# A split-fp32 input projection on TensorE: seven products of block sums in place of eight, in two halves of the contraction

## The chip, the cores and the metric

The kernel runs on one core of one Trainium2 chip. Times are device microseconds (us) of one execution. The core's engines each run their own instruction stream in order: TensorE (PE in the rows; PEld is its weight load), VectorE (DVE), ScalarE (ACT), GpSimd (POOL), and SyncE (SP), whose stream issues nearly all DMA transfers.

## The reference

One decoder layer for 1,024 tokens of width 2,048. A first product gives everything that two parallel branches need, and two more products and a layer norm close the layer. All of it is float32.

```python
mod = c @ w_ada[i] + b_ada[i]
shift, scale, gate = jnp.split(mod, 3, axis=-1)
h = _ln(x) * (1.0 + scale[:, None, :]) + shift[:, None, :]
proj = h @ w_in[i]
q, kv, ng, za, us, zb, ga, gb = jnp.split(proj, offs, axis=-1)
o_a = _nsa(q, kv, jax.nn.sigmoid(ng), rel_bias, ...) * jax.nn.silu(za)
o_b = _s5(us, ssm_a_re[i], ...) * jax.nn.silu(zb)
m = jax.nn.sigmoid(ga) * (o_a @ w_branch_nsa[i]) + jax.nn.sigmoid(gb) * (o_b @ w_branch_ssm[i])
x = _ln(DEEPNORM_ALPHA * x + gate[:, None, :] * (m @ w_out[i])) * ln_g[i] + ln_b[i]
```

`w_in` is 2,048 by 9,776: 76 tiles of 128 output columns, and 48 columns `ng`. `_nsa` is sparse attention (16 heads in 4 groups, compressed, selected and window parts), `_s5` a state-space layer (64 groups of 16 channels, an associative scan over the tokens).

## The kernel before, in words

**Number format.** Each float32 operand is split into a rounded `hi` (a cast on ACT) and the rest `lo` (a subtraction on DVE, L113). A product is three matmuls: hi x hi, hi x lo and lo x hi.

**Input projection.** `h` lies in SBUF, transposed, as 16 pairs of tiles `hhi[k]`, `hlo[k]` of 128 x 1,024. `dense` (L238) computes one tile of 128 output columns for all tokens in two PSUM banks (`dps`): four units of weights come in (`w_unit`, 256 KB each, split on ACT and DVE), each serves four `k`, and `mm6` issues six matmuls of 128 x 512 per `k`: 96 a tile. 73 tiles run so. Three more (`acc`) are accumulated in the startup, while `w_ada`'s shift and scale part (64 tiles `wa` of 512 KB) still arrives. `dense_ng` computes the 48 gate columns in 64 matmuls. An evacuation function per kind of tile (`ev_us`, `ev_q`, `ev_k`, `ev_v`, ...) writes the result to DRAM.

**Stages.** After the startup come eight state-space blocks (`Ssm.block`), each put behind two or three dense tiles; then `compress` (the compressed keys and values); then attention units (`Attention.unit`, one group of heads and one block of 128 queries). `EARLY` says how many of the eight query blocks of each group are computed early, on top of the dense tiles that are left; the other ones run late, on top of the output products. A scheduler orders the instructions of each engine by priority and by when buffers come free. Weights are loaded and split at a raised priority, so the dense matmuls fill the gaps of the other work.

**A state-space block** is a chain over the engines: `rot` (powers of a rotation, built by doubling on DVE), X (`sps<-U,et`, PE), rotations and scans on DVE, Y (`sps<-e,v`, PE), a trip of `y` through DRAM that reorders it (`y_d`, then the tile `gy`), the GELU, and the store of `U`. The tiles `rot0` and `rot1` have buffers of their own; `bank()` gives the block's PSUM tiles from a pool of four, which `ev_v` and `compress` use too.

Of the kernel before, what the change touches and what calls it, by code (L numbers as in the profile page):

```python
# [27 lines left out]
EARLY = (6, 6, 6, 4)  # L28
# [22 lines left out]
def _hybrid(es, tc, A, out):  # L51
# [33 lines left out]
    mb_d = [scratch(f"mb_d{i}", [128, 512]) for i in range(16)]  # L85

# [11 lines left out]
    stp = es.enter_context(tc.tile_pool(name="st", bufs=3))  # L98


    p1 = ExitStack()
    xh = p1.enter_context(tc.tile_pool(name="xh", bufs=32, side="right"))

    def w_unit(src, shape=[128, 4, 128], rp=None):

        raw = (rp or wp).tile([128, 512], F32, name="wraw", tag="wraw", bufs=3 if rp else WR)
        if len(shape) == 3:
            raw = raw.rearrange("p (k c) -> p k c", k=4)
        ld(raw, src)
        hi = wp.tile(shape, F32R, name="whi", tag="whi")  # L110
# [5 lines left out]
    hhi, hlo = [None] * KT, [None] * KT  # L116
    w_in = A["w_in"]

    def mm6(ps, k, hi, lo, ku):
        a = k == 0  # L120
        z = k == KT - 1
        for hf in range(2):
            c = slice(512 * hf, 512 * hf + 512)
            PE.matmul(ps[hf], hi[:, ku], hhi[k][:, c], start=a, stop=False)  # L124
            PE.matmul(ps[hf], hi[:, ku], hlo[k][:, c], start=False, stop=False)  # L125
        for hf in range(2):
            c = slice(512 * hf, 512 * hf + 512)
            PE.matmul(ps[hf], lo[:, ku], hhi[k][:, c], start=False, stop=z)  # L128

# [3 lines left out]
    sc_cm = tc.tile_pool(name="sc", bufs=1)  # L133
    sc = sc_cm.__enter__()
    cP = sc.tile([128, KT, 32], F32, name="cP")
    ld(cP, A["c"])
    ssm = Ssm(nc, tc, A, sc, ident, ld, rd, st_)
    sct_cm = tc.tile_pool(name="sct", bufs=1)
    sct = sct_cm.__enter__()
    s0 = ExitStack()  # L140
    p0 = s0.enter_context(tc.tile_pool(name="p0", bufs=1))
    pp = s0.enter_context(tc.tile_pool(name="pp0", bufs=1, space=PSUM))

    NS = 3
    units = []


    def load_wa(n):
        wa = (stp if n % 7 % 2 else p0).tile([128, 2, 512], F32, name="wa", tag="stg" if n % 7 % 2 else "wa", bufs=3 if n % 7 % 2 else 4)
        ld(wa, A["w_ss"][n // 8][:, 2 * (n % 8):2 * (n % 8) + 2])  # L150
        return wa

    xn, was = [], {}
    for b in range(NB):
        t = xh.tile([128, T], F32, name=f"xa{b}", tag="xh"), xh.tile([128, T], F32, name=f"xb{b}", tag="xh")
# [14 lines left out]
        if b > 1:  # L170
            was[b - 2] = load_wa(b - 2)
    xs = [(p0 if k == KT - 1 else xh).tile([128, T], F32, name=f"x{k}", tag="x15" if k == KT - 1 else "xh")
          for k in range(KT)]
    for hf in range(2):
        for k in range(KT):
            tp = pp.tile([128, 512], F32, name="tp", tag="st", bufs=6)
# [4 lines left out]
    for k in range(0, KT, 2):  # L181
        mp = pp.tile([128, 512], F32, name="mp", tag="mp", bufs=2)
        for n in range(8):
            wa = was.pop(4 * k + n) if 4 * k + n in was else load_wa(4 * k + n)
# [3 lines left out]
        pm = p0.tile([128, 512], F32, name="pm", tag="pm", bufs=1)  # L188
        S.copy(pm, mp)
        for i in range(4):  # L190
# [3 lines left out]
        if k % 4 == 0:  # L194
            units.append([w_unit(w_in[TILES["us"][i]][:, k:k + 4]) for i in range(NS)])

    acc = [[pp.tile([128, 512], F32, name="acc", tag="st", bufs=6) for _ in range(2)] for _ in range(NS)]
    for k in range(KT):
        V.tensor_scalar(xs[k], xs[k], mods[:, k, 0:1], mods[:, k, 1:2], op0=MUL, op1=ADD)
        hhi[k] = xh.tile([128, T], F32R, name=f"hhi{k}", tag="xh")  # L200
        S.copy(hhi[k], xs[k])
        hlo[k] = xh.tile([128, T], F32R, name=f"hlo{k}", tag="xh")
        V.tensor_tensor(hlo[k], xs[k], f(hhi[k]), op=SUB)
        for i in range(NS):
            mm6(acc[i], k, *units[k // 4][i], k % 4)

    ssm.tables(sct)


    def ev_us(ps, i):  # L210
        s = stage()
        sv_ = s.rearrange("p (s m) -> p s m", s=8)
        for hf in range(2):
            S.copy(sv_[:, :, 64 * hf:64 * hf + 64], ps[hf].rearrange("p (m s) -> p s m", s=8))
        st_(us_d[i].rearrange("s c g m -> (c g) s m"), sv_)

    for i in range(NS):
        ev_us(acc[i], i)
    s0.close()
    sct_cm.__exit__(None, None, None)  # L220

    psa = es.enter_context(tc.tile_pool(name="psa", bufs=2, space=PSUM))
    psb = p1.enter_context(tc.tile_pool(name="psb", bufs=2, space=PSUM))
    turn = [0]

    def psum_a():
        return psa.tile([128, 512], F32, name="pa", tag="d")

    def pair():
        turn[0] ^= 1  # L230
        return [(psa if turn[0] else psb).tile([128, 512], F32, name="dps", tag="d") for _ in range(2)]

    pss_cm = tc.tile_pool(name="pss", bufs=4, space=PSUM)
    pss = pss_cm.__enter__()

    side = iter(())

    def dense(wi, ev, *a):  # L238
        ps = pair()
        for u in range(4):  # L240
            with tc.high_priority(offset=WPRI):
                hi, lo = w_unit(w_in[wi][:, 4 * u:4 * u + 4])
            for ku in range(4):
                mm6(ps, 4 * u + ku, hi, lo, ku)
            next(side, None)
        ev(ps, *a)
# [4 lines left out]
    def ev_cin(ps, i):  # L251
        s = stage()
        v = s.rearrange("p (b m) -> p b m", b=16)
        for hf in range(2):
            S.copy(v[:, :, 32 * hf:32 * hf + 32], ps[hf].rearrange("p (m b) -> p b m", b=16))
        st_(cin_d[i], v)

    def ev_split(ps, scale):
        hi, lo = stage(F32R), stage(F32R)
        for hf in range(2):  # L260
            c = slice(512 * hf, 512 * hf + 512)
            S.mul(hi[:, c], ps[hf], scale)
            V.scalar_tensor_tensor(lo[:, c], ps[hf], scale, f(hi[:, c]), op0=MUL, op1=SUB)
        return f(hi), f(lo)

    def ev_q(ps, i):
        hi, lo = ev_split(ps, -0.125)
# [5 lines left out]
    def ev_k(ps, w, i):  # L273
        hi, lo = ev_split(ps, 1.0)
# [4 lines left out]
    def ev_v(ps, w, i):  # L279
        s = stage()  # L280
        for hf in range(2):
            S.copy(s[:, 512 * hf:512 * hf + 512], ps[hf])
        for hf in range(2):
            tp = bank()
            for b in range(4):
                PE.transpose(tp[:, 128 * b:128 * b + 128], s[:, 512 * hf + 128 * b:512 * hf + 128 * b + 128], ident[:, :128])
# [7 lines left out]
    def ev_silu2(ps, dst):  # L294
        s = stage()
        for hf in range(2):
            c = slice(512 * hf, 512 * hf + 512)
# [1135 lines left out]
```

## Time and profile before

| what | value |
|---|---|
| median of 3 runs | 3238.25 us (3235.42 to 3239.47) |
| the profiled execution's own time | 3234.84 us |
| span of its profile | 3233.1 us |
| PE busy | 3162.2 us, 98% |
| DVE busy | 1686.2 us, 52% |
| ACT busy | 1127.2 us, 35% |
| POOL busy | 85.5 us, 3% |
| moved by DMA | 432.21 MB, 134 GB/s over the span |

The shares are means over stages that differ: in a stage an engine can be full that is half idle over the whole. The granted clock of TensorE over the span is 0.991 of full speed.

### The profile page before, as it was taken

To read this page: it belongs to the slowest core of one execution; us is meant where nothing else is said; L and a number is where in the kernel's file an instruction comes from. 1 tells how busy PE (TensorE), PEld (TensorE's weight loads), DVE (VectorE), ACT (ScalarE), POOL (GpSimd) and SP (SyncE) were. 2 spreads that over 40 slices of the span, in tenths; PEclk is the share of its full clock that TensorE was granted. 3 is DMA by queue.
4 is the path that set the end of the run, shared out by engine and by line. 5 is a ranking of instruction groups with operands and counts; after the bars stand their busy time and mean duration, and the time that the engine had idled before them with its cause. 6 is when DMAs were issued, how large, how long until landed. Compare 5 with 4: busy or idle time off the path is not lost.

```text
span 3233.1 us, 43112 instructions
## 1 busy us (share of the span) xinstructions
PE 3162.2 (98%) x15603; PEld 2538.1 (79%) x15603; DVE 1686.2 (52%) x4615; ACT 1127.2 (35%) x2327; POOL 85.5 (3%) x66
## 2 busy tenths in 40 slices
PE   7999999999999999999999999999999999999896
PEld 4467788888888888888888888887888888788784
DVE  8354678763444434334333334426777665534737
ACT  4212222222433334333433234325555443322323
POOL 0000000000000000000000000000000000000302
PEclk9999999999999999999999999999999999999998
DMA  9654524344322232222322222236668444734533
GB/s 335 236 170 147 172 94 141 103 128 119 117 92 74 77 97 88 71 64 83 97 77 74 67 84 91 76 126 202 213 207 285 142 131 147 241 114 144 166 119 138
DMA packets 286398, 432.21 MB, mean 134 GB/s; under 512 B 40324, under 2 KB 139428, under 8 KB 286184
## 3 DMA queue, kind: packets, MB, share of 16 engines
q1 hardware_dynamic: 286184, 429.45, 41.0%
q8 instruction: 123, 2.02, 0.3%
q14 instruction: 91, 0.75, 0.1%
HBM read 331.30 MB, written 98.05 MB: 133 GB/s over the span
## 4 chain that ended last, share of the span: by engine, by line
PE 93%; DVE 3%; DMA 2%; ACT 1%; issue 1%; SPq 0%; ACTq 0%; DVEq 0%
PE dps L124 17%; PE dps L125 17%; PE dps L128 17%; PE po L957 5%; PE ps L814 4%; PE pt L935 4%; PE pa L462 4%; PE pa L463 4%; PE pa L464 4%; PE e L602 2%; PE e L601 2%; PE e L603 2%; PE mp L187 2%; DVE r L595 1%; PE acc L124 1%; PE e L462 1%
## 5 line engine op out<-in xcount | busy, mean ns | idle before, releaser
L124 PE MATMUL dps<-hhi,whi 128*128 128x512 f32 x2336 | 927.8, 397 | 0.0
L125 PE MATMUL dps<-hlo,whi 128*128 128x512 f32 x2336 | 925.2, 396 | 0.0
L128 PE MATMUL dps<-hhi,wlo 128*128 128x512 f32 x2336 | 750.3, 396 | 0.0
L111 ACT CAST whi<-wraw 128x512 fp32r<-128x512 f32 x544 | 336.2, 619 | 1054.9 <-PE dps L125 622.7
L113 DVE TENSOR_TENSOR wlo<-wraw,whi 128x512 fp32r<-128x512 f32 x544 | 381.0, 701 | 600.9 <-ACT whi L111 587.8
L124 PEld LDWEIGHTS dps<-hhi,whi 128*128 128x128 f32 x2336 | 439.7, 188 | 103.8 <-issue 13.0
L125 PEld LDWEIGHTS dps<-hlo,whi 128*128 128x128 f32 x2336 | 439.8, 188 | 93.7 <-issue 7.0
L128 PEld LDWEIGHTS dps<-hhi,wlo 128*128 128x128 f32 x2336 | 433.4, 188 | 92.5 <-issue 5.7
L940 DVE TENSOR_TENSOR ptl<-pt,pth 128x512 fp32r<-128x512 f32 (+2 forms) x320 | 204.1, 646 | 269.3 <-ACT pth L939 267.6
L939 ACT CAST pth<-pt 128x512 fp32r<-128x512 f32 (+2 forms) x320 | 172.0, 552 | 456.7 <-PE pt L935 456.0
L462 PE MATMUL pa<-op,whi 128*128 128x512 f32 x528 | 210.0, 400 | 2.1 <-ACT op L449 1.7
L463 PE MATMUL pa<-op,whi 128*128 128x512 f32 x528 | 209.7, 397 | 2.5 <-DMA op<-oa_d 2.5
L464 PE MATMUL pa<-op,wlo 128*128 128x512 f32 x528 | 208.8, 396 | 0.0
L602 PE MATMUL e<-wlo,m 128*128 128x512 f32 x368 | 148.0, 402 | 9.9 <-DVE rsd L42 5.4
L603 PE MATMUL e<-whi,m 128*128 128x512 f32 x368 | 146.3, 398 | 0.0
L929 ACT ACTIVATE psl<-psl,mn 128x128 f32<-128x128 f32 (+7 forms) x128 | 99.2, 775 | 81.3 <-DVE mn L842 80.5
L601 PE MATMUL e<-whi,m 128*128 128x512 f32 x368 | 122.0, 401 | 0.6 <-ACT whi L111 0.6
L462 PEld LDWEIGHTS pa<-op,whi 128*128 128x128 f32 x528 | 99.8, 189 | 23.3 <-ACT op L449 3.3
L463 PEld LDWEIGHTS pa<-op,whi 128*128 128x128 f32 x528 | 99.6, 189 | 22.9 <-DMA op<-oa_d 2.9
L464 PEld LDWEIGHTS pa<-op,wlo 128*128 128x128 f32 x528 | 99.6, 189 | 20.1 <-issue 0.7
L904 POOL TENSOR_TENSOR near<-bn,msk 128x512 f32<-128x512 f32 x32 | 35.1, 1098 | 2662.1 <-DVE msk L900 2535.9
L883 ACT ACTIVATE pw<-pw,mn 128x640 f32<-128x640 f32 (+4 forms) x128 | 88.9, 694 | 32.4 <-DVE mn L842 31.6
(308 smaller groups left out, 4271.1 us busy)
## 6 DMA issues: line engine op xcount, KB each, us to landing
wraw<-in_w_in SPq DMA_DIRECT2D x304, 256.0 KB, 3.0
wraw<-in_w_out SPq DMA_DIRECT2D x136, 256.0 KB, 3.0
wa<-in_w_ss SPq DMA_DIRECT2D x64, 512.0 KB, 5.7
wg<-in_w_gate SPq DMA_DIRECT2D x32, 512.0 KB, 3.6
q<-q_d SPq DMA_DIRECT2D x64, 256.0 KB, 4.1
wraw<-in_w_bn SPq DMA_DIRECT2D x64, 256.0 KB, 3.1
q_d<-stg SPq DMA_DIRECT2D x32, 256.0 KB, 3.9
oa_d<-ptl SPq DMA_DIRECT2D x64, 128.0 KB, 2.2
```

The source lines that it names most:

```text
L111: S.copy(hi, raw)
L113: V.tensor_tensor(lo, raw, f(hi), op=SUB)
L124: PE.matmul(ps[hf], hi[:, ku], hhi[k][:, c], start=a, stop=False)
L125: PE.matmul(ps[hf], hi[:, ku], hlo[k][:, c], start=False, stop=False)
L128: PE.matmul(ps[hf], lo[:, ku], hhi[k][:, c], start=False, stop=z)
L462: PE.matmul(ps, hi[:, j], x[k][0], start=k == 0, stop=False)
L463: PE.matmul(ps, hi[:, j], x[k][1], start=False, stop=False)
L464: PE.matmul(ps, lo[:, j], x[k][0], start=False, stop=k == 7)
L601: PE.matmul(a, mk[0][:, t], hi, start=k == 0, stop=False)
L602: PE.matmul(a, mk[0][:, t], lo, start=False, stop=False)
L603: PE.matmul(a, mk[1][:, t], hi, start=False, stop=k == KT - 1)
L940: V.tensor_tensor(lo[0:n, :w], tp[0:n, :w], f(hi[0:n, :w]), op=SUB)
```

## The change

Two output tiles and two tiles of `k` form blocks of a 2 x 2 product, with the two token halves as the other side. `dense(pair, half, last)` computes a pair of output tiles over one half of the contraction (8 of 16 `k`, four 2 x 2 blocks `j`) by seven products (`PRODUCTS`) of sums of weight blocks with sums of `h` blocks. The sums of `h` (`combine`) are formed once, 28 tiles `hc` of 512 KB for a half, and only one half's are in SBUF; both halves' lie in DRAM (`hc_d`), and `fetch_h` reads 28 of them over the 28 that are in use. The weight sums (`weights`) are formed for each pair and half on POOL, and each of the seven is split. The first half's result of a pair goes to DRAM (`pt_d`) and is read back and added by the second.

The order becomes: the startup forms scale and shift for half of `k`, and the other half between the first four pairs; 18 pairs `one` (us, the compress inputs, k, v, q, za) over half 0; `ng` and the position table; `fetch_h(1)`; the 18 pairs over half 1, with a state-space block behind every second of the first 16; `ng`; `compress`; then 20 pairs `two` over half 1, `fetch_h(0)`, and 20 over half 0, two steps to each of 20 early attention units. `EARLY` goes from 22 units to 20. `compress` splits its weights in the buffers of `dense`, and `rot` shares the buffer `gy`.

```diff
-EARLY = (6, 6, 6, 4)
+EARLY = (5, 5, 5, 5)
...
+    def fetch_h(half):
+        for i, _, _ in PRODUCTS:
+            for j in range(4):
+                d = hc[i, j] = hcp.tile([128, 2, 512], F32R, name="hc", tag="hc")
+                rd(f(d), hc_d[half][j][i])
+
+    def weights(wis, half):
...
+        P.tensor_tensor(s3, a11, a21, op=SUB)
+        yield w_split(a11)
+        P.tensor_tensor(a11, a22, s3, op=SUB)
+        yield w_split(a11)
+        P.tensor_tensor(a21, a21, a22, op=ADD)
+        yield w_split(a21)
+        yield w_split(s3)
+        P.tensor_tensor(a11, a12, a11, op=SUB)
+        yield w_split(a11)
+        yield w_split(a12)
+        yield w_split(a22)
+
+    def product(ps, i, hi, lo, first):
+        for j in range(4):
+            bh, bl = hc[i, j][:, 0], hc[i, j][:, 1]
+            PE.matmul(ps, hi[:, j], bh, start=first and j == 0, stop=False, skip_group_check=True)
+            PE.matmul(ps, hi[:, j], bl, start=False, stop=False, skip_group_check=True)
+            PE.matmul(ps, lo[:, j], bh, start=False, stop=j == 3, skip_group_check=True)
+
+    def dense(pair, half, last):
...
+        for n, (i, b, first) in enumerate(PRODUCTS):
+            with tc.high_priority(offset=WPRI):
+                hi, lo = next(w)
+            if first:
+                ps[b] = dbank()
+            product(ps[b], i, hi, lo, first)
+            if n == 1:
+                S.copy(s1, ps["a"])
+                if last:
+                    u2 = acc()
+                    V.tensor_tensor(u2, ps["b"], s1, op=ADD)
+                    P.tensor_tensor(c12, c12, u2, op=ADD)
...
+    for n in range(n_one):
+        dense(one[n], 1, True)
+        if n % 2:
+            b = n // 2
+            if b < 8:
+                ssm.block(sp, bank, b, us_d[b], y_d[b], y2_d[b], stage)
...
+        work = [(p, 1, False) for p in two]
+        work += [None] + [(p, 0, True) for p in two]
...
+            att.unit(qb)
+            while n < (u + 1) * len(work) // len(early):
+                step()
...
-        R = [tl(f"rot{i}", [128, 4, 128]) for i in range(2)]
+        rot = tl("gy", [128, 2, 4, 128])
+        R = [rot[:, i] for i in range(2)]
```

Before, PE's stream through a state-space block (here from one block's X, `sps<-U,et`, past its Y, `sps<-e,v`, to the first row of the next block) reads so; every `dps` row is a dense matmul:

```order
L1266 MATMUL sps<-ident,ka 128x128 [waits DVE_49]
...
L1274 MATMUL sps<-U,et_3557 64x128 x7
L128 MATMUL dps<-hhi_1135,wlo 128x512 x2
...
L1320 MATMUL sps<-U,w_3581 128x128 [waits Activation_49]
L128 MATMUL dps<-hhi_1158,wlo 128x512 x2
L124 MATMUL dps<-hhi_1181,whi 128x512
...
L1321 MATMUL sps<-e_3676,v_3538 128x127 [waits DVE_49]
...
L124 MATMUL dps<-hhi_1388,whi 128x512
...
L1252 MATMUL sps<-ident,e_4025 128x128 x3
```

After, the stretch from block 1's Y (`v_5595`) through the whole of block 2 (`e_6091` to `v_6100`) and block 3 up to its X (`et_6638`), to the transposes of `ev_v` (`sps<-ident,stg`), reads so. The rows left out are rows of the same lines:

```order
L210 MATMUL dps<-hc,wlo 128x512
L1462 MATMUL sps<-e_5732,v_5595 128x127 [waits DVE_49]
...
L1392 MATMUL sps<-ident,e_6091 128x128 [waits DVE_49]
...
L1414 MATMUL sps<-U,et_6118 64x128 [waits DMAHW3_49,PE_49]
...
L1462 MATMUL sps<-e_6236,v_6099 128x127 [waits DVE_49]
...
L1392 MATMUL sps<-ident,e_6611 128x128 [waits DVE_49]
...
L1414 MATMUL sps<-U,et_6638 64x128 [waits DMAHW3_49,PE_49]
...
L371 MATMUL sps<-ident,stg 128x128 [waits DMAHW7_49,DVE_49,PE_49]
...
L208 MATMUL dps<-hc,whi 128x512
```

Of its 84 rows none is a dense matmul: what stood between the blocks has moved ahead of the first row and behind the last. The same holds from the last `ng` matmul (L409) on: the rest of block 6, all of block 7 and all of `compress` (L834 to L862) stand in 152 rows without a dense one.

```order
L409 MATMUL dps<-hc,whl 128x512 x25
L1462 MATMUL sps<-e_8368,v_8231 128x127 [waits DVE_49]
...
L1392 MATMUL sps<-ident,e_8731 128x128 [waits DVE_49]
...
L1414 MATMUL sps<-U,et_8758 64x128 [waits DMAHW1_49,PE_49]
...
L1462 MATMUL sps<-e_8876,v_8739 128x127 [waits DVE_49]
...
L836 MATMUL sps<-cth,wlo 128x264
L208 MATMUL dps<-hc,whi 128x512 [waits Activation_49]
```

Before, the matmuls of the last block and of `compress` stand in pieces of at most 24 rows between dense rows. At the end of the early attention, too, the order moves: before, 161 dense matmuls stand behind the last row of the last early unit; after, the last dense row stands ahead of 274 rows of the last four early units, and then the output products begin (`pa<-op`).

On SP, `fetch_h(1)` stands behind the partial sums' stores; `hc<-hc_d` are its transfers, `wr` the weights, `wg` another weight:

```order
L261 DMA pt_d_274<-stg 128x1024 [waits DMAHW1_49,DVE_49,Pool_49]
L182 DMA hc<-hc_d_0_245 128x1024 [waits DMAHW2_49,PE_49]
L182 DMA hc<-hc_d_1_246 128x1024 [waits DMAHW3_49,PE_49]
L182 DMA hc<-hc_d_2_247 128x1024 [waits PE_49]
L182 DMA hc<-hc_d_3_248 128x1024 [waits DMAHW5_49,PE_49]
L456 DMA wg<-in_w_gate 128x4x256 [waits DMAHW7_49,DMAHW6_49]
L456 DMA wg<-in_w_gate 128x4x256 [waits DMAHW1_49]
L189 DMA wr<-in_w_in 128x1024 [waits DMAHW0_49,DVE_49,Pool_49]
```

Each `hc` transfer waits for PE to be done with the tile that lies in its buffer. Before, there is no such row: `hhi` and `hlo` stay where they are.

## Rows read from the trace of the kernel before

**Rows 1.** The page: busy time and share, busy tenths of 40 slices.

```profile
PE 3162.2 (98%) x15603; PEld 2538.1 (79%) x15603; DVE 1686.2 (52%) x4615; ACT 1127.2 (35%) x2327; POOL 85.5 (3%) x66
...
DVE  8354678763444434334333334426777665534737
```

**Rows 2.** Busy time by stretch: stretch, length, PE, PEld, DVE, ACT, POOL, clock, DMA share, GB/s.

```profile
0.00:160.00 160.00, 140.28 (x659) 70.54 (x660) 99.52 (x393) 54.69 (x86) 0.20 (x4) 0.98 0.82 287
0.00:40.00 40.00, 20.28 (x112) 12.27 (x114) 32.62 (x103) 18.98 (x33) 0.20 (x4) 0.96 0.92 341
220.00:700.00 480.00, 480.00 (x2704) 377.90 (x2704) 339.42 (x850) 109.27 (x191) 0.00 (x0) 1.00 0.42 132
780.00:2180.00 1400.00, 1400.00 (x6835) 1160.56 (x6835) 539.83 (x1718) 503.19 (x1174) 13.59 (x12) 1.00 0.26 85
```

**Rows 3.** Timeline of PE: start, duration, line, tile.

```profile
1900.62 0.39 PE L124 MATMUL dps<-hhi,whi 128*128 128x512 f32 x1
...
1901.53 0.63 PE L128 MATMUL dps<-hhi,wlo 128*128 128x512 f32 x2
```

**Rows 4.** DVE's and PE's groups from 220 to 700 us: busy, mean ns.

```profile
L113 DVE TENSOR_TENSOR wlo<-wraw,whi 128x512 fp32r<-128x512 f32 x70 | 48.2, 688 | 38.1 <-ACT whi L111 37.1 <-issue 0.3
L263 DVE SCALAR_TENSOR_TENSOR stg<-dps,stg 128x512 fp32r<-128x512 f32 x10 | 6.5, 682 | 0.0
...
L124 PE MATMUL dps<-hhi,whi 128*128 128x512 f32 x558 | 222.4, 399 | 0.0
...
L365 PE MATMUL sps<-wg,cP 128*32 128x256 f32 x232 | 18.5, 391 | 0.0
```

**Rows 5.** Timeline of DVE, one block's X to the next one's X.

```profile
511.98 0.69 DVE L1193 TENSOR_TENSOR t<-sps,rot 128x512 f32<-128x512 f32 x1 [2.18 <-PE sps L1274]
...
524.89 0.69 DVE L1193 TENSOR_TENSOR e<-t,t 64x512 f32<-64x512 f32 x1
...
541.41 1.23 DVE L1193 TENSOR_TENSOR w<-gy 128x1024 f32<-128x1024 f32 x1 [1.77 <-DMA gy<-y_d]
...
544.70 0.24 DVE L1193 TENSOR_TENSOR t<-rot,up 128x4 f32<-128x4 f32 x2
...
548.20 2.25 DVE L1338 SCALAR_TENSOR_TENSOR U<-w,gy 128x1024 f32<-128x1024 f32 x1
...
560.53 0.42 DVE L1193 TENSOR_TENSOR rot<-t,t 128x256 f32<-128x256 f32 x1
...
563.96 0.69 DVE L1193 TENSOR_TENSOR t<-sps,rot 128x512 f32<-128x512 f32 x1 [2.16 <-PE sps L1274]
```

**Rows 6.** Timelines of SP and PE: last block's store, first matmul of `compress`.

```profile
718.33 0.33 SPq L1340 DMA_DIRECT2D y_d<-U  x1
757.73 0.28 PE L694 MATMUL sps<-cth,cwh 128*128 128x264 f32 x1
```

**Rows 7.** Timelines of DVE and POOL near 3030 us.

```profile
3022.11 4.79 DVE L595 TENSOR_TENSOR r<-r,ln_g 128x512 f32<-128x512 f32 x4
3033.74 1.57 DVE L113 TENSOR_TENSOR wlo<-wraw,whi 128x512 fp32r<-128x512 f32 x1
3037.11 0.67 DVE L113 TENSOR_TENSOR wlo<-wraw,whi 128x512 fp32r<-128x512 f32 x1
3023.01 13.43 POOL L596 TENSOR_TENSOR r<-r,ln_b 128x512 f32<-128x512 f32 x8 [325.34 <-DVE r L595]
```

**Rows 8.** First and last dense matmul (durations in ns, then starts in us).

```profile
L124 PE MATMUL dps<-hhi,whi x2336: 387/392/796, 182.8 to 2178.6; 128*128 128x512 f32 x195
```

**Rows 9.** Timeline of PE in the startup.

```profile
33.20 1.05 PE L187 MATMUL mp<-wa,cP 128*32 128x512 f32 x4
```

**Rows 10.** DVE's and PE's groups from 780 to 2180 us.

```profile
L113 DVE TENSOR_TENSOR wlo<-wraw,whi 128x512 fp32r<-128x512 f32 x208 | 144.3, 694 | 330.1 <-ACT whi L111 321.4 <-DMA op<-oa_d 4.8 <-PE dps L128 1.8
...
L124 PE MATMUL dps<-hhi,whi 128*128 128x512 f32 x1662 | 658.2, 396 | 0.0
```

**Rows 11.** PE's waits where the late units begin (2180 to 2200 us).

```profile
PE ps L814 <- DMA kw<-k_d: 4.8, 1, 4.8
```

More of the change, by code (lines that the diff above doesn't have):

```diff
@@ L144, in _hybrid, with load_wa @@
[L144 to L150, printed above, removed]
+    pp = s0.enter_context(tc.tile_pool(name="pp0", bufs=2, space=PSUM))
+    n_wa = [0]
+    def load_wa(j, n):
+        n_wa[0] += 1
+        wa = stp.tile([128, 2, 512], F32, name="wa", tag="stg")
+        ld(wa, A["w_ss"][j][:, 2 * n:2 * n + 2])
@@ L207, in _hybrid @@
[L207 to L246, printed above, removed]
+        for k in (2 * j, 2 * j + 1):
+            V.tensor_scalar(xs[k], xs[k], mods[:, k, 0:1], mods[:, k, 1:2], op0=MUL, op1=ADD)
@@ L256, in ev_cin, with ev_split @@
         st_(cin_d[i], v)
[L258 to L267, printed above, removed]
+    def ev_split(y, scale):
+        hi = stage(F32R)
+        S.mul(hi, y, scale)
+        lo = y.bitcast(F32R)
+        V.scalar_tensor_tensor(lo, y, scale, f(hi), op0=MUL, op1=SUB)
+        return f(hi), y
@@ L277, in ev_k, with ev_v @@
             st_(k_d[w][2 * i + j][1], lo[64 * j:64 * j + 64])
[L279 to L282, printed above, removed]
+    def ev_v(y, w, i):
         for hf in range(2):
@@ L308, in dense_ng @@
[L308 to L322 removed]
+        S.activation(s, y, AF.Tanh, scale=0.5)
@@ new lines, in ev_silu2, with ev_tanh, dense_ng @@
+        V.scalar_tensor_tensor(y, s, 1.0, y, op0=ADD, op1=MUL)
+        st_(dst, y)
+    def ev_tanh(y, dst):
+        S.activation(y, y, AF.Tanh, scale=0.5)
+        st_(dst, y)
+    def dense_ng(half, last):
+        raw = wk.tile([128, 8, 64], F32, name="wng", tag="wr")
+        ld(raw, A["w_ng"][:, 8 * half:8 * half + 8])
+        hl = []
+        for i in range(2):
+            t = wp.tile([128, 4, 128], F32R, name="whl", tag="whi")
+            S.copy(t[:, :, 0:64], raw[:, i::2])
+            V.tensor_tensor(t[:, :, 64:128], raw[:, i::2], f(t[:, :, 0:64]), op=SUB)
+            hl.append(t)
+        s = stage()
+        if last:
+            rd(s, png_d)
+        for c, ops in ((lh, ((0, B11), (1, B21))), (rh, ((0, B11), (0, T1), (1, B22)))):
+            ps = dbank()
+            n = 0
+            for i, x in ops:
+                for j in range(4):
+                    for part in range(2):
+                        n += 1
+                        PE.matmul(ps, hl[i][:, j], hc[x, j][:, part], start=n == 1, stop=n == 8 * len(ops))
+            if last:
+                V.tensor_tensor(s[:, c], ps, s[:, c], op=ADD)
+            else:
+                S.copy(s[:, c], ps)
+        if not last:
+            st_(png_d, s)
+            return
@@ L378, in _hybrid @@
     jobs = []
-    for i in range(NS, 8):
+    for i in range(8):
         jobs.append((TILES["us"][i], ev_us, i))
```

302 lines of the change are left out of this document (188 added, 114 removed).

## The prediction, made before the changed kernel was run

> **What bounds the kernel now.** I read the page first. TensorE is busy 98% of the span, VectorE 52%, with slices of 3 to 8 tenths [rows 1]. So the kernel ends when TensorE has worked through its list, and VectorE's mean says little, because its load is uneven. The table by stretch shows how uneven: from 220 to 700 us, where the state-space blocks run, VectorE is busy 339 of 480 us, and from 780 to 2180 us 540 of 1,400, with TensorE full in both [rows 2]. The timeline of TensorE then gives the price of a matmul: four starts lie 0.91 us apart [rows 3], so 0.2275 us each. (The durations of about 0.39 us overlap.) A matmul that goes saves 0.2275 us only while something else is ready behind it. Whether half of the dense matmuls can still cover the blocks is what the rest is about.
>
> **What is removed.** Before: 7,008 dense matmuls in `dps` (73 x 96), 288 in the startup and 64 for `ng`. After: 76 pair-halves of 7 x 4 x 3 = 84, so 6,384, and 80 for `ng`. That is 896 fewer, times 0.2275 us = **204 us**. A pair-half is 84 x 0.2275 = 19.1 us of TensorE.
>
> **What VectorE gets.** A pair-half with `last` has seven splits at 0.69 us and six additions out of PSUM, priced like the evacuation at 0.68 [rows 4]: 9 us. The evacuations of the 36 tiles of the 18 pairs add some 28 us (about 40 operations of that size). The state-space blocks keep their operations: 339 us [rows 2] less 48 of splits and about 12 of evacuations [rows 4] is some 280 us for seven and a half blocks, so 37 us each. TensorE's share of a block follows in the same way: 480 us less 3 x 558 dense matmuls, 381 us, and 18.5 for `wg` [rows 4] leaves 80, some 10 us a block. In the second run over the 18 pairs VectorE therefore has 18 x 9 + 28 + 8 x 37 + about 12 for `compress` = 498 us, and TensorE 18 x 19.1 + 8 x 10 + 24 for `compress` (its 24 us are 192 matmuls at half a dense one's price, an estimate) = 448 us. **VectorE has 50 us too much even if it never waits.** That is the lower bound of this stage. In the same stretch before it had 140 us to spare [rows 2].
>
> **Where it shows, place by place.** The upper side comes from the order of instructions, with the length of a block from the trace. One block's cycle there is 52 us from X to X, with dense splits between, and with `rot` of the next block begun at 544.7, ahead of this one's last operation at 548.2 [rows 5]. Now `rot` shares the buffer of `gy` and must follow that operation. The links are [rows 5]: X to the last rotation 13.6 us; from there to the first use of `gy`, the trip through DRAM, 15.8, of which I take 13.5 without the splits between; to the end of the last operation 9.0, of which 7 without the early `rot`; `rot` from there to 560.95, 10.5; to the next X 3.0. That is some 48 us, of which TensorE works 10.
> - Between block 1's Y and block 3's X no dense row stands: 1.75 cycles, 84 us, less 17 of TensorE's work, **67** (45 if VectorE's 37 a block set the pace; 90 with contention).
> - The eight pairs after that, with 2.4 blocks' worth of VectorE's work by the order: VectorE 8 x 9 + 14 + 2.4 x 37 = 175 us and 35 of delay by POOL (below), TensorE 153 + 24. That is 33 too much, of which splits made ahead take some: **24** (0 to 50).
> - After the last pair: block 7 whole, 48 - 10, and the end of block 6, some 8; then `compress`. Before, its first matmul came 39 us after the last block's store [rows 6], under dense tiles. Nothing covers it now, but the loads that it waits for no longer queue among weights: I take 31. **77** in sum (55 to 100).
>
> **What POOL adds.** Four to seven additions of 128 x 512 a pair-half. The trace of before has POOL beside VectorE: eight took 13.43 us, 1.7 each, while VectorE's four took 4.79, 1.2 each, and a split took 1.57 us there and 0.67 just after [rows 7]. So an operation of VectorE that meets one of POOL's loses up to 0.9 us. I count 35 us for the SSM stage above (40 or so meetings) and nothing elsewhere, since VectorE has room there.
> The Trainium skill, SBUF — State Buffer, "Who interferes with whom", says that a VectorE instruction with two SBUF inputs contends with a GpSimd instruction that reads SBUF, over one shared port pair that is an exclusive lock. The trace agrees in that both slow down [rows 7]; by the rule alone each of POOL's 70 additions in the ten pairs with blocks 2 to 6 could hold VectorE for its whole length, 119 us at 1.7.
>
> **Fetches.** `fetch_h(1)` moves 28 x 0.52 = 14.7 MB, and some 6 MB of partial sums and weights queue among it. At 287 to 341 GB/s, two early stretches of before [rows 2], 20.7 MB take 61 to 72 us. It can start some 5 us before `ng` ends, since the first buffer is used up to then; the first pair covers 19. **38** (22 to 50). `fetch_h(0)` moves 18 MB or so, 53 to 63 us, but its order fits the order in which the pair ahead of it gives up the tiles (16 us earlier), and attention (12 us a unit, below) lies between: **14** (0 to 30).
>
> **Startup.** Dense work began at 182.8 us [rows 8], after 288 matmuls, 65.5 us: as if at 117. Now x, half of `wa`, weights and the stores of the first `hc` come first, 35 MB by the order, 103 to 122 us at the same rates, and some 10 for the last scale, shift and sums. The second half of the scale and shift matmuls, 64 at 0.26 us [rows 9], 16 us, moves behind it, and its 17 MB of `wa` with the stores are barely covered by four pairs. **30** (15 to 45).
>
> **End of the early attention.** From 780 to 2180 us TensorE had 3 x 1,662 dense matmuls [rows 10], 1,134 of 1,400 us, so some 12 us for each of 22 units; VectorE 540 us [rows 2] less 144 of splits [rows 10] and some 25 of evacuations, 17 us each. Dense work now ends four units early: 4 x 17 = 68 us of VectorE against some 45 of TensorE, and without filler the chain score, maximum, exponent, transpose, product shows too. **38** (20 to 60). Two more late units: before, their first wait was 4.8 us [rows 11]; **5** (0 to 25).
>
> **Sum.** 30 + 38 + 14 + 67 + 24 + 77 + 38 + 5 = 293 us of new waiting against 204 saved: +89. The profiled execution took 3234.84 us, 3.4 below the median, so 3324; I take **3325**, 2.7% above the median. All lower ends give 157 (3188), all upper 450 (3481). The ends are independent in part, so this case's own range is 3268 to 3382.
>
> **Rivals.**
> *VectorE alone sets the middle stage.* If the blocks overlap better than their links say, the three middle terms (168) fall to the 50 that VectorE has too much. With the other terms as forecast (125) that is 3235 - 204 + 175 = 3206, faster; with the lower ends of the startup, the fetches and the tail 3143. It decides from the point where the three cost less than 204 - 125 = 79. For it: VectorE was idle 140 us in that stage before, so the chains do leave room. Against it: 84 and 152 rows of TensorE's list without a dense one, and an engine works its list in order.
> *POOL's additions hold VectorE.* In the ten pairs with blocks 2 to 6, 70 additions at up to 1.7 us are up to 119 us in place of 35, and splits that come late stop TensorE in other pairs too, where 1 us a pair-half in half of the 76 would be 38: +38 to +122, about 3405 in the middle. For it the slower operations beside POOL [rows 7]; against it that many of VectorE's operations read PSUM, and that weights are split ahead of their use.
> That the matmuls don't go is excluded by the order, where they are counted.
>
> **How the numbers follow.** A measurement here tells 0.2% (6.5 us) from no change. The forecast has 0.70, the first rival 0.16, the second 0.14. The first rival ends faster (0.15, and 0.01 within 0.2%); the forecast's low end gives 0.03 to faster and 0.03 to the same. Faster 0.18, same 0.04, slower 0.78. For 8 in 10 I cut about a tenth at each end: 3205, in the first rival, to 3412, in the second.
>
> **What would show it.** Right: dense matmuls 0.2275 us apart; TensorE idle some 67 us in one stretch between two blocks and 77 from the second `ng` to the end of `compress`, with VectorE or a transfer as what it waits for; waits on `hc<-hc_d` of some 38 and 14 us; gaps in the four units ahead of the output products. Wrong: TensorE above 95% busy in the second run over the 18 pairs (first rival), or waits on `whi` and `wlo` spread over all pairs, with VectorE's operations at 1.2 us and more beside POOL's (second).

## The result, and the profile after

The changed kernel takes 3478.48 us (median of 4 runs, 3476.44 to 3480.82), the kernel before 3237.53 us on the same chips: a ratio of 1.0745 (95% interval 1.0726 to 1.0763). It is slower by 241 us. The prediction said 3325 with a range up to 3412: the sign was right, the size too small by a factor of 2.8, and the time lies outside the range.

The first rows come from the page of the changed kernel: busy times, then 40 slices of the span for TensorE, VectorE and the granted clock.

```profile
span 3479.0 us, 43926 instructions
PE 3091.2 (89%) x14683; PEld 2433.9 (70%) x14683; DVE 2255.1 (65%) x5251; ACT 1359.8 (39%) x2668; POOL 778.7 (22%) x554
...
PE   6898999885588549999999999978999999899896
...
DVE  6445333898899946656656766845787766544746
...
PEclk9898999998699869999999999958999999999998
```

Beside [rows 1], TensorE falls from 98% to 89%, VectorE rises by 569 us of busy time, and POOL from 85.5 to 778.7 us. The row of the clock had only nines and one 8 before; now it falls to 5 and 6 tenths where TensorE has its longest gaps, in the 11th, 15th and 27th slice. The dense matmuls themselves do what was forecast. In the timeline of TensorE (start, duration, line) they follow each other at 0.23 us, as in [rows 3], and the profile counts 6,384:

```profile
2100.62 0.40 PE L208 MATMUL dps<-hc,whi 128*128 128x512 f32 x1
2100.85 0.39 PE L209 MATMUL dps<-hc,whi 128*128 128x512 f32 x1
2101.08 0.39 PE L210 MATMUL dps<-hc,wlo 128*128 128x512 f32 x1
2101.31 0.39 PE L208 MATMUL dps<-hc,whi 128*128 128x512 f32 x1
```

So 204 us went, and some 445 came (241 + 204). The table by stretch shows where (columns as in [rows 2]): the swap of halves (545 to 615 us), the 18 pairs with the state-space blocks and `compress` (615 to 1288), the early attention with dense work (1288 to 2244), its last four units without any (2244 to 2386), and the rest.

```profile
0.00:240.00 240.00, 191.28 (x847) 107.53 (x848) 115.28 (x209) 78.72 (x136) 61.25 (x47) 0.94 0.80 286
240.00:545.00 305.00, 288.70 (x1328) 216.54 (x1327) 141.16 (x189) 94.42 (x163) 112.92 (x80) 0.96 0.56 197
545.00:615.00 70.00, 65.60 (x264) 43.91 (x263) 26.18 (x50) 16.51 (x23) 18.15 (x15) 0.95 0.88 337
615.00:834.00 219.00, 186.70 (x855) 142.14 (x853) 202.25 (x535) 72.69 (x99) 82.63 (x56) 0.96 0.41 133
834.00:934.00 100.00, 30.14 (x211) 25.95 (x212) 85.84 (x217) 13.60 (x23) 2.68 (x2) 0.60 0.21 70
934.00:1164.00 230.00, 199.93 (x988) 156.42 (x987) 217.92 (x395) 68.83 (x109) 84.14 (x55) 0.95 0.49 163
1164.00:1288.00 124.00, 46.16 (x273) 41.09 (x272) 73.91 (x145) 23.02 (x34) 3.94 (x3) 0.67 0.30 83
1288.00:2244.00 956.00, 945.50 (x4556) 778.72 (x4555) 622.65 (x1551) 467.80 (x1039) 334.64 (x243) 0.99 0.44 148
2244.00:2386.00 142.00, 98.61 (x335) 68.42 (x333) 72.69 (x275) 61.11 (x147) 2.10 (x2) 0.60 0.28 77
2386.00:3479.00 1093.00, 1038.56 (x5042) 853.23 (x5041) 697.23 (x1694) 463.09 (x899) 76.25 (x54) 0.98 0.52 167
```

VectorE is busy 580 of the 673 us from 615 to 1288, 86%. That is uneven: 92% up to 1164 us (202.25 + 85.84 + 217.92 of 549), and 60% in the last 124 us, where the last block and `compress` stand; TensorE's own busy time is no measure of work where the clock is 0.60, since its matmuls last longer there. The count of dense matmuls is. The same table for the tile `dps` alone (the count behind TensorE's time is that of its matmuls, `ng` included):

```profile
0.00:240.00 240.00, 106.43 (x399) 74.96 (x400) 11.71 (x17) 8.36 (x15) 0.94 0.80 286
240.00:545.00 305.00, 269.89 (x1098) 210.04 (x1097) 37.12 (x54) 21.78 (x38) 0.96 0.56 197
545.00:615.00 70.00, 53.70 (x208) 39.31 (x207) 7.39 (x11) 2.92 (x5) 0.95 0.88 337
615.00:834.00 219.00, 173.63 (x681) 129.61 (x679) 30.60 (x45) 4.66 (x8) 0.96 0.41 133
834.00:934.00 100.00, 0.00 (x0) 0.00 (x0) 0.69 (x1) 0.00 (x0) 0.60 0.21 70
934.00:1164.00 230.00, 176.23 (x685) 131.94 (x686) 34.01 (x51) 4.68 (x8) 0.95 0.49 163
1164.00:1288.00 124.00, 9.25 (x42) 7.39 (x41) 2.66 (x4) 0.00 (x0) 0.67 0.30 83
1288.00:2244.00 956.00, 836.15 (x3358) 614.52 (x3359) 136.26 (x199) 46.43 (x80) 0.99 0.44 148
```

Taking 0.2275 us for each dense matmul off the length of a stretch, and TensorE's other work as the prediction counted it (10 us a block, 12 a unit), leaves what was lost there. Two counts differ from it. `compress` has 107 matmuls (3 x 32, 3 and 8), not 192, so 12 us and not 24. And the late units have more matmuls than the mean early one: TensorE does 239 more of them after 2386 us than before did from 2180 on (5,042 against 4,803) and is busy 35 us more (1038.56 against 1003.75), where the prediction's price for two units gives 24. "Other" is what stands in the stretch by the order; the figures in the last column are worked out in this way and good to some 5 us each.

| stretch | length - dense - other | predicted | lost |
|---|---|---|---|
| startup and half 0, to 545 | 545 - 341 - 18 (`wg`), less the 117 of before | 30 | 69 |
| swap of halves, 545 to 615 | 70 - 47 - 11 (position table) | 38 | 12 |
| 615 to 834 | 219 - 155 - 18 | 0 | 46 |
| block 1's Y to `ev_v`, 834 to 934 | 100 - 0 - 17 | 67 | 83 |
| 934 to 1164 | 230 - 156 - 25 | 24 | 49 |
| to the end of `compress`, 1288 | 124 - 10 - 26 | 77 | 88 |
| early attention, with `fetch_h(0)` | 956 - 764 - 16 x 12 | 14 | 0 |
| last four early units | 142 - 0 - 48 | 38 | 94 |
| two more late units | (1093 - 1053) - 35 | 5 | 5 |

The 1053 are the time of before from 2180 us to the end. The sum is 446 against 293 predicted; 446 - 204 = 242. The profiled executions differ by 3480.82 - 3234.84 = 246.

Two groups of waits tell who was late in the stretch without dense work from 834 to 934 us (what waited, for what, total, times, longest):

```profile
POOL stg L234 <- DMA stg<-pt_d: 94.9, 1, 94.9
PE sps L1414 <- DMA U<-us_d: 33.9, 2, 17.7
PE sps L1462 <- DVE e L1333: 20.0, 2, 10.1
```

TensorE waits for the block's own chain there (the second and third line): for `U` of the next block, which is loaded into the buffer that the last one's result leaves, and for VectorE's `e`. Dense work is held by the partial sum that is to be read into a stage tile (94.9 us, the first line); the stage tiles are held by the results of `ev_v`, whose transposes stand behind block 3's PSUM tiles.

In the stretch before it, from 615 to 834 us, dense work does stand in TensorE's list, and TensorE's longest waits are for what VectorE makes for it, the `lo` halves of the weights and the sums out of PSUM:

```profile
PE dps L210 <- DVE wlo L118: 11.4, 10, 2.3
PE dps L208 <- DVE acc L233: 7.3, 5, 3.0
```

### The profile page after: what moved, and what is told of

It reads as the page before. It is cut to its first block, busy times and chain, and to the rows that moved or that the text cites. A ratio compares the mean times of both kernels' runs of the same rounds, so it can differ in the third digit from the quotient of the medians.

```text
span 3479.0 us, 43926 instructions
## 1 busy us (share of the span) xinstructions
PE 3091.2 (89%) x14683; PEld 2433.9 (70%) x14683; DVE 2255.1 (65%) x5251; ACT 1359.8 (39%) x2668; POOL 778.7 (22%) x554
## 5 line engine op out<-in xcount | busy, mean ns | idle before, releaser
L208 PE MATMUL dps<-hc,whi 128*128 128x512 f32 x2128 | 865.8, 407 | 59.4 <-ACT stg L230 16.1
L210 PE MATMUL dps<-hc,wlo 128*128 128x512 f32 x2128 | 847.4, 403 | 17.4 <-DVE wlo L118 17.4
L209 PE MATMUL dps<-hc,whi 128*128 128x512 f32 x2128 | 853.6, 401 | 1.2 <-DVE hc L166 1.1
L116 ACT CAST whi<-wr 128x512 fp32r<-128x512 f32 x456 | 280.4, 618 | 681.2 <-PE dps L209 483.3
L208 PEld LDWEIGHTS dps<-hc,whi 128*128 128x128 f32 x2128 | 408.9, 192 | 183.3 <-issue 25.1
L210 PEld LDWEIGHTS dps<-hc,wlo 128*128 128x128 f32 x2128 | 408.0, 192 | 121.4 <-DVE wlo L118 30.0
L118 DVE TENSOR_TENSOR wlo<-wr,whi 128x512 fp32r<-128x512 f32 x456 | 365.0, 802 | 192.1 <-ACT whi L116 175.2
L209 PEld LDWEIGHTS dps<-hc,whi 128*128 128x128 f32 x2128 | 408.9, 192 | 92.5 <-issue 6.7
L118 DVE TENSOR_TENSOR wlo<-wraw,whi 128x512 fp32r<-128x512 f32 x240 | 170.8, 713 | 178.3 <-ACT whi L116 178.0
L116 ACT CAST whi<-wraw 128x512 fp32r<-128x512 f32 x240 | 148.2, 619 | 315.9 <-PE e L743 116.7
L245 POOL TENSOR_TENSOR stg<-stg,acc 128x512 f32<-128x512 f32 x76 | 116.5, 1533 | 365.3 <-DVE acc L244 281.3
L743 PE MATMUL e<-whi,m 128*128 128x512 f32 x368 | 145.8, 396 | 0.0
```

Of the source, the lines that this page charges most:

```text
L208: PE.matmul(ps, hi[:, j], bh, start=first and j == 0, stop=False, skip_group_check=True)
L209: PE.matmul(ps, hi[:, j], bl, start=False, stop=False, skip_group_check=True)
L210: PE.matmul(ps, lo[:, j], bh, start=False, stop=j == 3, skip_group_check=True)
L743: PE.matmul(a, mk[1][:, t], hi, start=False, stop=k == KT - 1)
```

## The experiments

Each is one run with one time, beside a run of the kernel before on the same chip (3237.05 to 3241.24 us). Differences are against the changed kernel's 3478.5; its own runs spread over 4.4 us, and 13 came out 14 us longer by a stage that its edit doesn't touch, so I read nothing into less than 15. The length of the run with the blocks, where it is given, is from the last matmul of the position table (L440) to the last product of `compress` with `w_k2` (L862): 674 us in the changed kernel.

**1. POOL's additions left out.** The sums of weight blocks and POOL's additions to the results are left out, in both halves:

```diff
-        P.tensor_tensor(s3, a11, a21, op=SUB)
         yield w_split(a11)
-        P.tensor_tensor(a11, a22, s3, op=SUB)
...
-                    u2 = acc()
-                    V.tensor_tensor(u2, ps["b"], s1, op=ADD)
-                    P.tensor_tensor(c12, c12, u2, op=ADD)
+                    V.tensor_tensor(c12, ps["b"], s1, op=ADD)
...
```

> This kernel leaves out the weight-block sums on POOL (the seven splits of a pair-half then work on unsummed blocks) and POOL's three additions in the second half (VectorE writes its sum directly), so POOL is idle in the dense work, with the same number of VectorE, ScalarE and TensorE instructions; its output is not the reference's. Rival 'POOL's additions hold VectorE': VectorE's split goes from 802 ns back to about 690, the run over the 18 pairs with state-space blocks (615 to 1288 us) gets 60 to 120 us shorter, total about 3370 to 3420. Theory 'lost cover and full VectorE': POOL is worth no more than the 35 us that I counted, total 3440 or more.

Measured: 3405.40, -73 us. The run with the blocks is 57 us shorter and ends near 1208 instead of 1288 us; half 0 gives another 24, and a few are lost again behind. In VectorE's groups from 615 to 1300 us (busy, mean ns), the split of the changed kernel comes first, then two of its other operations, then the split without POOL (more of them, because that window reaches 92 us into the next stage) and one of the same operations:

```profile
L118 DVE TENSOR_TENSOR wlo<-wr,whi 128x512 fp32r<-128x512 f32 x101 | 84.0, 836 | 5.0 <-ACT whi L116 4.9
L1333 DVE TENSOR_TENSOR e<-t,t 128x512 f32<-128x512 f32 (+1 forms) x64 | 51.5, 805 | 5.6 <-PE sps L1462 4.5
L1333 DVE TENSOR_TENSOR t<-sps,gy 128x512 f32<-128x512 f32 x32 | 20.5, 682 | 0.5
```

```profile
L118 DVE TENSOR_TENSOR wlo<-wr,whi 128x512 fp32r<-128x512 f32 x136 | 93.3, 687 | 18.7 <-ACT whi L116 17.0 <-PE dps L205 1.2
L1322 DVE TENSOR_TENSOR e<-t,t 128x512 f32<-128x512 f32 (+1 forms) x64 | 43.9, 686 | 4.8 <-PE sps L1451 3.8
```

Operations with both inputs in SBUF take 805 and 836 ns beside POOL and 686 without it; the one that reads PSUM (`sps`) takes 682 beside POOL. The rival had the total right, and the stage 3 us short of its 60 to 120; the theory's bound of 3440 fell.

**2. More dense work at the end of the early attention.**

```diff
+        for p in two[-4:]:
+            dense(p, 0, True)
```

> The last four pairs' products over half 0 are computed a second time behind the last early attention unit: 336 more dense matmuls, 76 us of TensorE at 0.2275 us, and their splits. If the 141 us without dense rows before the output products is a chain that TensorE's idle slots only lengthen (cover theory), the added work hides in it: total within -10 to +20 us of 3478, and the granted clock there goes from 0.57 to 1.00. If the stretch is limited by the work of TensorE or VectorE, the time goes up by 60 to 80 us, to about 3550.

Measured: 3529.62, +51 us for 76 us of TensorE's work: between the two. The stretches of this run, with the added work and without any (columns as before):

```profile
2244.00:2340.00 96.00, 94.65 (x458) 77.31 (x457) 77.20 (x180) 50.20 (x108) 33.97 (x24) 1.00 0.45 141
2340.00:2428.00 88.00, 61.03 (x198) 42.60 (x197) 41.75 (x158) 34.52 (x79) 2.10 (x2) 0.57 0.41 108
```

The dense work isn't spread over the four units: it runs ahead of them as before, covers one and a half, and 88 us stay bare, again at a clock of 0.57. My picture that the gaps would swallow it all was wrong; a unit that is covered costs TensorE 12 us, a bare one 35 (142 / 4).

**3. 17 early units.**

```diff
-EARLY = (5, 5, 5, 5)
+EARLY = (5, 4, 4, 4)
```

> EARLY = (5, 4, 4, 4): 17 early attention units in place of 20, 15 late in place of 12. Theory 'the early units have too little dense work over them, the late ones have room': the 141 us without dense rows shrink to about 40, total about 3390. Rival 'a unit takes its own chain of some 57 us wherever it runs' (16 units in 958 us before the dense work ends): what is saved early comes back in the late stage, 3 x 50 us, total 3460 to 3540.

Measured: 3437.03, -41, between the two. The bare stretch falls from 142 to some 20 us, all of it one wait for the late units' first keys (`kw<-k_d`, 20.3 us). The rest (2254 to the end) takes 1181 us where it took 1093, 29 us for each of three more late units, so about two thirds of the gain comes back:

```profile
2254.00:3435.00 1181.00, 1106.88 (x5418) 907.95 (x5418) 771.73 (x1996) 519.98 (x1042) 83.20 (x60) 0.98 0.50 160
```

Of these 88 us, 68 are TensorE's own busy time (1106.88 against 1038.56): the units that move are the fifth of their groups and have 125 matmuls each (376 for three), where the 16 covered early ones have 75. Some 20 are more waiting. So a late unit costs mostly its own work; the lack of cover is the smaller part.

**4. `rot` and `U` freed.**

```diff
-        rot = tl("gy", [128, 2, 4, 128])
+        rot = tl("rot", [128, 2, 4, 128])
...
-        o = tl("U", [128, T])
+        o = stage()
```

> rot gets a buffer of its own, and the block's result goes into a stage tile, so that the next block's U can be loaded before this one's is stored. By the order the longest stretches without a dense row fall from 132 and 177 rows to 107. Theory 'the chain of a block without cover sets windows B and D' (my prediction's step): 100.7 us and 115 us fall to some 60 and 70, total 3380 to 3410. Rival 'VectorE is full there anyway' (87 to 98% busy from 650 to 1200 us): only the part in which VectorE waits comes back, 20 to 45 us, total 3435 to 3460.

Measured: 3512.14, +34: both theories miss. The run with the blocks is 26 us longer. A stretch of 88 us without dense work appears at 643 us, in which the longest wait is again

```profile
POOL stg L234 <- DMA stg<-pt_d: 74.9, 1, 74.9
```

The block's result now takes one of the four stage tiles of the dense work, so dense pairs behind a block wait for its end. That is a tie that the experiment itself brought in; it says nothing on `rot`, and was taken apart in 13.

**5. Tables early.** The block `ssm = Ssm(...)`, `ssm.tables(sct)` moves from behind `fetch_h(1)` into the run over half 0, behind the fourth sum of h.

> The state-space tables (Ssm.tables) are computed in the run over half 0, behind the fourth sum of h, in place of behind fetch_h(1). Theory 'VectorE is full from 615 to 1290 us, and the tables that used to run in the startup are part of it, a term that I had left out': 45 to 50 us of VectorE go to a stage where it is 40% busy, total 3430 to 3450. Rival 'the chains of the blocks without cover set the time': the tables stand ahead of them, total 3465 to 3485.

Measured: 3445.90, -33, as the first theory had it. The run with the blocks takes 46 us less, and 6 us come back in half 0. In the kernel before, these tables ran in the startup, between 40 and 105 us, where VectorE was busy 77% with them.

**6. More cover.** 10 pairs over half 0, then these and 8 more over half 1, `fetch_h(0)`, the 8 over half 0; a block behind every third.

```diff
...
+    steps = [(p, 1, True) for p in one[:na]] + [(p, 1, False) for p in one[na:]] + [(p, 0, True) for p in one[na:]]
+    for n, s in enumerate(steps):
+        if n == n_one:
+            with tc.high_priority(offset=WPRI):
+                fetch_h(0)
+        dense(*s)
...
```

> Only the first 10 of the 18 pairs run over half 0 before the swap. Then come these 10 over half 1, the other 8 over half 1, fetch_h(0), and these 8 over half 0: the eight blocks are spread over 26 pair-halves in place of 18, and a third fetch is paid. Theory 'VectorE is full': 8 pair-halves more bring 153 us of TensorE's work into the stage and 69 us of VectorE's, less some 10 for the fetch: -60 to -90 us, total 3390 to 3420. Rival 'chains without cover': the order has no stretch over 56 rows without dense work before compress, so windows B and the waits around it go altogether, -150 us, total about 3330.

Measured: 3447.85, -31: less than either. The sums of h and the stores of both halves now fall into six pairs, and TensorE waits 33 us there for the copy of `dps` to a stage tile; and VectorE is busy 348 of 400 us in the new stretch, 87% as before.

**7. Cover, tables and 17 units together.**

> The two changes before together with 17 early units, EARLY = (5, 4, 4, 4), which by themselves gave -41 us. If the three gains add: 3478 - 75 - 40 - 41 = about 3320 (3295 to 3350), still slower than the kernel before. If the stage is no longer VectorE's after the reorder, the tables bring nothing more: about 3360.

Measured: 3371.60, -107. The three single gains give 33 + 31 + 41 = 105: they add. (The expected 3320 had put 75 on the cover, which brought 31.)

**8. Rotation powers left out** (two fills stand in their place).

> The powers of the rotation (rot) are not computed: two fills stand in their place, 42 small VectorE operations and 10.6 us fewer in each of the 8 blocks; the output is not the reference's. Theory 'VectorE is full in the whole stage': nearly all of the 85 us come back, total 3395 to 3420. Theory 'the chain of a block counts only in the stretches without dense work' (my prediction's): 10.6 us for each of 2.75 blocks, total 3445 to 3455.

Measured: 3433.51, -45, between the two and all of it in the run with the blocks. That is more than the 29 of the chain where nothing covers it, and half of VectorE's 85. VectorE's load counts beyond the stretches without cover, and not for its full length.

**9. POOL's additions moved to VectorE.** All of them, as

```diff
-        P.tensor_tensor(s3, a11, a21, op=SUB)
+        V.tensor_tensor(s3, a11, a21, op=SUB)
```

> POOL's additions of the dense work (four to seven a pair-half) are done by VectorE instead. In the run over the 18 pairs with blocks VectorE gets 18 x 7 x 0.69 = 87 us more and meets no POOL. Theory 'each of POOL's additions costs VectorE nearly as long as doing it itself' (leaving them out gave -60 us in that stage): the stage grows by 15 to 35 us, the run over half 0 changes by -10 to +10, total 3470 to 3510. Rival 'POOL costs VectorE little, and leaving the sums out helped by shortening the way of the weights': the stage grows by 60 to 87 us, total 3540 or more.

Measured: 3478.84, +0.4. The total lies in the first theory's range, but the stage does not grow by 15 to 35 us: the run with the blocks lasts 676 us (674 without the edit). Its table row, from where the stage begins in this run to where it ends, and the split's:

```profile
603.00:1277.00 674.00, 457.78 (x2319) 370.39 (x2318) 560.29 (x1404) 180.24 (x264) 0.00 (x0) 0.83 0.40 125
```

```profile
L118 DVE TENSOR_TENSOR wlo<-wr,whi 128x512 fp32r<-128x512 f32 x101 | 68.6, 683 | 4.9 <-ACT whi L116 4.5
```

VectorE does 116 additions more in that run, 79 us, and is busy 560 us where it was 580. So POOL's help cost VectorE more than the work that it took over. The +0.4 hides two changes. Half 0 is 12 us shorter, and the dense work ends 26 us earlier, at 2218 us; but the units without dense work then take longer, 163 us for 142:

```profile
2218.00:2381.00 163.00, 115.31 (x374) 79.64 (x372) 82.33 (x326) 71.74 (x183) 2.10 (x2) 0.57 0.26 73
```

**10. and 11. The kernel of 7 with the sums on VectorE, and with the edit of 4.**

> The kernel with more cover, early tables and 17 early units (3371.6), with POOL's additions moved to VectorE. Its blocks lie over 26 pair-halves, where VectorE is 87% busy: 26 x 4.8 = 125 us more for VectorE against some 85 lost to POOL now. If VectorE's sum sets that stage, total +20 to +60, 3390 to 3430; if TensorE's list does, within 10 of 3372.

> The same kernel (3371.6) with rot and U in buffers of their own, which by itself cost 34 us on the changed kernel. Theory 'VectorE's sum sets the stage, and freed chains only move the blocks forward': within 3355 to 3410. Theory 'with more cover the chains are what is left': 3320 to 3345.

Measured: 3349.15, 22 us faster than 7, against both expectations; and 3450.04, 78 us slower than 7, slower than either theory has it, with the wait of 4 again (`POOL stg L234 <- DMA stg<-pt_d`, 135 us in six times from 490 to 800 us).

**12. The transposes of v in other PSUM banks.**

```diff
     def ev_v(y, w, i):
         for hf in range(2):
-            tp = bank()
+            tp = psum_a()
```

> The transposes of ev_v write to the dense work's other PSUM pool and no longer stand behind the blocks' banks. By the order the 100 us without dense rows between blocks 1 and 3 are gone, and the last one (the rest of the blocks and compress) has 289 rows in place of 177. Theory 'VectorE's sum sets the whole stage': dense work only runs ahead, and the blocks are left over at the end, total 3455 to 3485. Theory 'single stretches without cover' (my prediction's): the 85 us of the stretch come back, less some 40 behind, total 3420 to 3440.

Measured: 3488.31, +10: 3 us above the first theory's range, 48 above the second's. This is the run that decides. The stretch from 834 to 934 us, which had no dense matmul, now has 281; the last stretch before the next pairs goes from 124 to 214 us. Both in the table by stretch, all instructions:

```profile
834.00:934.00 100.00, 84.45 (x393) 66.28 (x392) 94.95 (x166) 26.42 (x42) 35.85 (x24) 0.91 0.49 154
1081.00:1295.00 214.00, 73.16 (x468) 65.67 (x467) 149.54 (x350) 33.92 (x52) 1.43 (x2) 0.64 0.23 69
```

What was lost between the blocks is lost behind them. The run with the blocks ends at 1295 us (1288 without the edit). VectorE is busy 434 of the 465 us up to 1081, 93%, and 150 of 214 behind. So the blocks come no faster with dense work between them, and what is left of them stands at the end, where TensorE has nothing else.

**13. `rot` alone.** Only the first half of the edit of 4.

> rot alone gets a buffer of its own; U and the stage tiles stay. Theory 'VectorE's sum sets the stage': 3465 to 3485. Theory 'the chain of a block counts where nothing covers it': 10 us for 2.75 blocks, 3445 to 3455. If the stage tile was what made the run with rot and U slower, nothing of its +34 is seen here.

Measured: 3492.25, +14, a little above either expectation. The run with the blocks lasts 677 us and ends at 1287, within 1 us of the changed kernel's, and the output products begin at 2385.6 (2385.8 without the edit); the difference (12 us between the profiled executions) arises behind that, where the edit changes nothing. So the buffer that `rot` shares costs nothing, and the slowdown of that stage in 4 (701 us against 674) came from the stage tile, as far as the two runs tell it.

**14. All gains.** The kernel of 10 with the edit of 12, and `compress` with split tiles of its own.

> More cover, early tables, 17 early units, sums on VectorE (3349 so far), and now v's transposes in the other banks and compress with split tiles of its own; by the order no stretch of over 40 rows without dense work is left before the output products. The stretches of 23, 50 and 75 us without dense work hold some 25 us of TensorE's own work, so at most 120 us can come back; VectorE is 83% busy there and leaves about 60: 3285 to 3320. The kernel before (3238) is not reached.

Measured: 3298.55, as expected: 180 us faster than the changed kernel and 57 slower than before (3241.24 beside it). Its stage with blocks (490 to 1170 us) shows TensorE nearly full again, and VectorE at 90%:

```profile
490.00:1170.00 680.00, 627.12 (x3175) 498.30 (x3175) 611.04 (x1304) 226.81 (x351) 0.00 (x0) 0.96 0.54 179
```

Against 10 it is 51 us faster; which of the two new edits gave that was not separated (on the changed kernel the first one gained nothing, 12). No version tried here beats the kernel before.

## Why the prediction was wrong

**What held.** The 204 us, the price of a matmul, the sign, the direction of nearly every term, the two late units (5 and 5), and, within 11 us, the stretch around `compress` (77 predicted, 88 lost, at 107 matmuls where the prediction counted 192). The fetches were less than forecast: 12 and about 0 for 38 and 14. The first ran at 337 GB/s, near the top of my two rates, and the position table's 11 us of matmuls, which I had not counted as cover, lay beside it; the second is hidden under attention, all but some 8 us (TensorE is busy 42.1 of the 50 us from 1750 to 1800).

**The step that failed first is "What VectorE gets".** It gave VectorE 498 us of work in the run with the blocks and called 50 us too much the lower bound. VectorE was busy 580 us. Two terms were missing or too small. The tables, which had run in the startup, were left out altogether (5: -33 us of the kernel's time, 46 of the stage). And POOL's additions were priced at 35 us; leaving them out takes 57 us from the stage and 73 from the kernel (1), and 580 us of busy time fall to 495. That is the second rival's mechanism, which had a chance of 0.14. The rest of the sum was right: VectorE's operations of the stage, added up by their durations (which overlap a little, so this is more than busy time), take 539 us in 1, of which 41 are the tables; that leaves 498, to the microsecond only by luck, since 121 of the 126 splits fall into the stage. In the changed kernel they take 623, so POOL costs 84. TensorE's side, 448, was 12 too high, by the matmuls of `compress`.

**The step that was wrong in kind is "Where it shows, place by place".** It summed stretches without dense work, as if each were a cost of its own, and put nothing on the first pairs. The 100 us between blocks 1 and 3 were there as forecast (83 lost for 67), and the reason too: rows of TensorE's list without a dense one. But 12 removed that stretch and the time stayed, because the loss moved behind the last pair; 13 freed `rot` and gained nothing. VectorE's load sets the stage up to 1164 us, where it is busy 92% of the time; the losses of 46 and 49 us in the stretches on both sides, 0 and 24 in the prediction, are the same shortage, as TensorE's waits for `wlo` and `acc` show. Only in the last 124 us, with VectorE at 60%, I read the chain without cover as what sets the time, as the prediction had it; TensorE's longest wait there is 30.8 us for the first `whi` of `compress` (L834). And it isn't a sum alone: when VectorE's busy time falls, the stage falls by no fixed share of it (1: 85 us less busy, 57 off the stage; 8: 65 and 45; 5: 28 and 46; 9: 20 and none). What keeps VectorE from the last tenth, and whether other orders could fill it, stays open; in 14, with more cover, it reaches 90%.

**The end of the early attention was mis-sized,** 94 for 38. I had priced a unit at VectorE's 17 us and put some chain on top. A bare unit takes 35 us, with VectorE, ScalarE and TensorE all partly idle, so I put it down to the chain from engine to engine. TensorE's clock may be part of it: it was granted at 0.60 there, and a matmul of `po<-pth,vs` takes 442 ns where it takes 296 in the late units. How much of the 94 the clock makes was not separated. The last units stand bare because the dense work left for this stage (3,358 matmuls, where 780 to 2180 us had 4,986 before [rows 10]) is used up at the pace of one unit for some 210 of them.

**The startup and half 0** cost 69 for 30; leaving POOL's additions out gives back 24 of it (1). The trace names 16 us of TensorE's waits for copies into stage tiles and 24 us for the normalized x (`xn`) in the startup, where before had 2; how much of these was hidden was not separated.

The first rival (VectorE alone sets the stage) had the mechanism right in part, and its price wrong, since it took the 50 us for all that VectorE had too much. The second had the row that counted: POOL's 115 additions of the stage took 173 us and cost VectorE 84, and done by VectorE itself they take it 79 (9). ([rows 7] show only VectorE's slowdown. In the same trace POOL's `near<-bn,msk` takes 1.05 us, and 1.70 where it meets two of VectorE's operations.) The Trainium skill, SBUF — State Buffer, "Who interferes with whom", says that a VectorE instruction with two SBUF inputs contends with a GpSimd instruction that reads SBUF, over one shared port pair that is an exclusive lock. The runs agree with the contention, at about half of POOL's time. The prediction named that rule and gave the row the greater weight; with the 119 us that the rule gave it for the ten pairs in place of 35, it would have stood near 3408.

## What to carry to other kernels

Work that is full cover for something else has a second price: before shortening it, add up what each helper engine must do inside the shortened stretch, all that moves into it included, and compare that sum with the new length. A stretch without cover in the list of the main engine isn't a cost of its own while the helper that it waits for is full on both sides of it; take the stretch away and see whether the time goes or moves. Moving two-input additions from a busy VectorE to GpSimd bought nothing here: with them back on VectorE the kernel took the same time, and a better arranged one (7 and 10) got 22 us faster.

## What the runs showed of the hardware

- Beside POOL's additions, two groups of VectorE's two-input operations from SBUF took 805 and 836 ns where they take 686; one that reads PSUM took 682. POOL took 1.37 to 1.61 us for an addition that VectorE does in 0.68. With the 116 additions of that stage moved to VectorE, its busy time there fell from 580 to 560 us.
- In the three stretches without dense work the granted clock was 0.60 to 0.67. In the first and the last of them TensorE is shown busy 30.1 and 98.6 us for 17 and 48 us of work (an estimate, at the prices of covered blocks and units). The clock is not all of that, since durations that overlap in a full stream stand apart there.
